# The memory's mean squares by one-column products on TensorE instead of token-major loads

## Chip, cores and metric

The kernel runs on one core of a Trainium2 chip. The metric is the device time of one execution in microseconds. A time quoted here is the median of several runs; the profile belongs to one further execution, with its own time.

## The reference

A two-layer encoder over 1024 tokens of width 1024, with 256 memory tokens of the same width. Both layers read the memory through an RMS norm with a gain and one projection for keys and values:

```
def rmsnorm(x, g):
    y = x * rsqrt(mean(x * x, axis=-1) + EPS)
    return y * g

memn = rmsnorm(mem, mem_norm_gain)
for l in range(DEPTH):
    h = rmsnorm(x, norm_gain[l])
    mk, mv = split(memn @ w_mem_kv[l])      # 4 heads of 128 each
    ...                                     # projections of h, attentions, gate, output projection
return rmsnorm(x, final_norm_gain)
```

The part that matters here is the mean of `mem * mem` over the 1024 features, one number for each of the 256 memory tokens.

## The kernel before

The kernel is written against a framework that allocates tiles from pools and orders each engine's queue ahead of time. A pool tag has a fixed number of buffers (`xt` has three, `x` six, `wraw`, `wh` and `wl` four, the PSUM bank `tr` three); a new tile of a tag waits until the oldest one has been read for the last time. Each engine works off its queue in order. Loads are issued by SP, one queue for all of them, which stops when its next load has to wait for a buffer.

All of the change lies in the preparation, `project_a`, the first 130 us or so. Matmuls work on operands that are split into a high part and a rest (`wh` and `wl`, `ah` and `al`, `H`), three products for one. What happens there, in the order of the program:

- `quarter(q, ...)` loads the input feature-major, 256 tokens at a time, in four loads of 128 x 512 (two blocks of 128 features), and splits each with its gain (ACT makes the high part, DVE the rest). Quarters 0 to 3 are the tokens of x, quarter 4 is the memory, from `mq`.
- `a_unit` (L864) multiplies a quarter by the first weights; four units, one for each quarter, with no norm applied yet.
- `mem_keys` (L568) multiplies the memory by the key weights of layer 0 in two PSUM banks, `pj` and then `tr`, each from four weight tiles. `wparts` loads such a tile into `wraw`; ACT makes `wh` from it and DVE `wl`.
- `mem_values` (L597) does the same for the values.
- `rstd(io["mt"], ...)` (L814, L815) computes the memory's norm: the memory is loaded a second time, token-major, in four tiles of 128 x 512 (`xt`), ACT squares each with a sum along the row, DVE adds the two halves, and `inv_sqrt` makes `rs_m`. The norm is applied after the products, when the banks of keys and values are read.
- `a_weights(1)` loads the next weights, the first two tiles of them into `x` buffers; `stats` does for x what `rstd` does for the memory, with eight tiles of `xt` for each half of x.

A loop of the same kind as the new one stands at L283 (`rstd_cols`), much later: the squares' sum over features is a product with the column `inv_d`, which holds 1/1024.

The queues around the place are not written by hand: the framework's scheduler sets them from its own estimates of time, so a change at one place moves rows at others.

Of the kernel before, what the change touches and what calls it, by code (L numbers as in the profile page):

```python
# [12 lines left out]
AF = mybir.ActivationFunctionType  # L13
OP = mybir.AluOpType
# [5 lines left out]
D = 1024  # L20
KT = 8
MEM = 256
EPS = 1e-6
# [41 lines left out]
class Trunk:  # L65
# [881 lines left out]
    def project_a(self, qa, ks, v, qd, mem_h, kvd):  # L947


        nc, tc, io = self.nc, self.tc, self.io  # L950

        def quarter(q, parts, kps=range(4)):
            for kp in kps:
                x = self.st("x", [128, 2, 256], pool=self.xp)
                src = io["xq"][q, kp] if q < 4 else io["mq"][kp]
                loaded = nc.sync.dma_start(x, src.rearrange("p (a n) -> p a n", a=2))
                for i in range(2):
                    kt = 2 * kp + i
                    self.with_gain(x[:, i, :], kt + (0 if q < 4 else 16), *parts(kt))
            return loaded  # L960

        def tokens(q):
            return lambda kt: tuple(t[kt][:, q * 256:(q + 1) * 256] for t in self.h)
        late = []

        def after(end):

            late.append(end)
            if len(late) > 1:
                flush()  # L970

        def flush():
            with tc.issue_after(self.last.ins):
                late.pop(0)()

        warm = self.st("rp", [128, 512], F32R)
        self.st("so", [128, 512])
        self.st("rt1", [128, 512])
        nc.gpsimd.memset(warm.bitcast(F32), 0.0)
        nc.scalar.activation(self.rs_m, warm.bitcast(F32)[:, :2], AF.Sqrt)  # L980
        p = [self.ps("pj") for _ in range(2)]
        for i in range(9):
            nc.tensor.matmul(p[i % 2], warm[:, :128], warm, start=True, stop=True)
        w0, w1m = io["w_mem0"], io["w_mem1"]
        mem_l = self.st("mem", [128, KT, MEM], F32R, pool=self.xp)
        mem = [[t[:, i, :] for t in mem_h for i in range(4)], [mem_l[:, i, :] for i in range(KT)]]
        ws = self.a_weights(0, lambda kp: quarter(0, tokens(0), [kp]))
        units = []
        for q in range(4):
            units.append(self.a_unit(ws, q))  # L990
            if q < 3:
                quarter(q + 1, tokens(q + 1))
        self.loaded = quarter(4, lambda kt: (mem[0][kt], mem[1][kt]))
        for q, a in enumerate(units):
            units[q] = self.st("x", [128, 2, 256], pool=self.xp)
            self.copy(units[q], a)
        self.wsplit = ("act", "dve")
        end = [self.mem_keys(w0, mem, kvd[0], ("pj", "tr"), "so", "rt1")]
        self.wsplit = ("act", "both")
        end.append(self.mem_values(w0, mem, kvd[0], "so"))  # L1000
        self.rope_tables()
        vm = self.st("xv", [128, 2])
        self.loaded = self.raws[6]
        self.rstd(io["mt"], [0, 1], vm, self.rs_m)
        self.wsplit = ("act", "dve")
        w1 = self.a_weights(1)
        self.stats(range(4))
        self.loaded = None
        self.along_columns(self.rows_m, self.rs_m)
        for e in end:  # L1010
            e()
        for q in range(2):
            after(self.k_unit(units[q], q, ks, v))
        self.mem_keys(w1m, mem, kvd[1], ("tr", "tr"), "so", "rt1")()
        self.stats(range(4, 8))
        for q in range(2, 4):
            after(self.k_unit(units[q], q, ks, v))
        for q in range(4):
            after(self.q_unit(self.a_unit(w1, q), q, 0, qa, qd))
        w2 = self.a_weights(2)  # L1020
        self.along_columns(self.rows, self.rs)
        for q in range(4):
            after(self.q_unit(self.a_unit(w2, q), q, 2, qa, qd))
            if q == 1:
                self.mem_values(w1m, mem, kvd[1], "so")()
        while late:
            flush()
        return self.mem_q(io["w_e"], E_QM)
# [1142 lines left out]
def _perm():  # L2171
    t = np.arange(T).reshape(16, 8, 8)
    return t.transpose(1, 0, 2).reshape(-1)


def _constants():
    c = {"c_ident": np.eye(128, dtype=np.float32)}

    t = _perm()
    freqs = np.power(np.float32(10000.0), -np.arange(16, dtype=np.float32) / np.float32(16)).astype(np.float32)  # L2180
    cos = np.zeros((T, 64), np.float32)
    sin = np.zeros((T, 64), np.float32)
    for a, pos in ((0, t // 64), (32, t % 64)):
        ang = (pos.astype(np.float32)[:, None] * freqs).astype(np.float64)
        cos[:, a:a + 16] = cos[:, a + 16:a + 32] = np.cos(ang)
        sin[:, a:a + 16] = -np.sin(ang)
        sin[:, a + 16:a + 32] = np.sin(ang)
    cos, sin = cos[:, _HALVES], sin[:, _HALVES]
    c["c_cos"] = cos.reshape(8, 128, 64).transpose(1, 0, 2).copy()
    c["c_sin"] = sin.reshape(8, 128, 64).transpose(1, 0, 2).copy()  # L2190
    return c
# [7 lines left out]
def layout(i):  # L2199
    a = {k: np.asarray(v) for k, v in i.items()}  # L2200
    perm = _perm()
    x = a["x"][0]
    d = _constants()
    d["xT"] = np.ascontiguousarray(x[perm].T).reshape(8, 128, T)
    d["xt"] = x[perm].reshape(8, 128, D)
    d["mt"] = a["mem"][0].reshape(2, 128, D)
    d["mq"] = a["mem"][0].T.reshape(4, 2, 128, MEM).transpose(0, 2, 1, 3).reshape(4, 128, 2 * MEM)
    g = np.concatenate([a["norm_gain"].reshape(16, 128), a["mem_norm_gain"].reshape(8, 128),
                        a["final_norm_gain"].reshape(8, 128)])
    d["gains"] = np.ascontiguousarray(g.T)  # L2210
    d["w_e"] = _tiles(a["w_in_even"][0])
    d["w_o"] = _tiles(a["w_in_odd"][0])
    rows = lambda w: w.reshape(12, 128, D)[list(ROWS)].reshape(-1, D)
    wv = a["w_in_odd"][0][:, 128 * O_V:128 * O_QM]
    d["w_v"] = wv.reshape(KT, 128, 2, 512).transpose(2, 0, 1, 3)
    d["w_oe"] = _tiles(rows(a["w_out_even"][0]))
    d["w_oo"] = _tiles(rows(a["w_out_odd"][0]))
    d["w_mem0"] = _tiles(a["w_mem_kv"][0])
    d["w_mem1"] = _tiles(a["w_mem_kv"][1])
    g = [a[nm][0] for nm in ("k_norm_a", "q_norm_a")]  # L2220
    d["g_kq"] = np.stack([v for u in g for v in (u, u.reshape(2, 2, 16)[:, ::-1].reshape(64))])[None][:, :, _HALVES]
    d["sink_b"] = a["sink_b"].reshape(1, 8)


    rel = np.arange(384)[None, :] - 128 - np.arange(128)[:, None]
    n = np.abs(rel)
    nf = np.maximum(n, 1).astype(np.float32)
    large = 8 + (np.log(nf / np.float32(8)) / np.float32(np.log(16.0)) * np.float32(8)).astype(np.int32)
    bucket = np.where(rel > 0, 16, 0) + np.where(n < 8, n, np.minimum(large, 15))
    padded = lambda t: np.concatenate([t, np.full((len(t), 1), NEG, np.float32)], 1)  # L2230
    d["band"] = padded(a["rel_bias"].T)[:, np.where(n <= 128, bucket, 32)]
    p = np.arange(128)
    r, cc = p // 8, p % 8
    start = np.clip(r - 4, 0, 8)
    row = (r[None, :] >= start[:, None]) & (r[None, :] < start[:, None] + 8)
    at = np.zeros((128, 5, 128), np.int64)
    for i, (b, k) in enumerate(((7, 6), (3, 2), (3, 3), (3, 4), (0, 1))):
        cq, ck = 8 * b + cc, 8 * k + cc
        start = np.clip(cq - 8, 0, 48)
        ok = row & (ck[None, :] >= start[:, None]) & (ck[None, :] < start[:, None] + 16)  # L2240
        at[:, i] = np.where(ok, (7 - r[:, None] + r[None, :]) * 31 + 15 - cq[:, None] + ck[None, :], 15 * 31)
    d["offsets"] = padded(a["rpb_c"][0].reshape(16, 15 * 31))[:, at]

    d["xq"] = d["xT"].reshape(4, 2, 128, 4, 256).transpose(3, 0, 2, 1, 4).reshape(4, 4, 128, 512)
    we = a["w_in_even"][0]
    halves = lambda w: w.reshape(D, -1, 64)[:, :, _HALVES].reshape(D, -1)
    wa = np.concatenate([halves(we[:, 128 * E_KA:128 * E_VA]), we[:, 128 * E_VA:128 * E_QB],
                         halves(we[:, :128 * E_KA])], 1)
    d["w_a"] = wa.reshape(4, 2, 128, 3, 256).transpose(3, 0, 2, 1, 4).reshape(3, 4, 128, 512)
    return {k: np.ascontiguousarray(v) for k, v in d.items()}  # L2250
# [17 lines left out]
```

## Time and profile before

| | |
|---|---|
| runs | 1478.82, 1481.55, 1482.13 us (median 1481.55) |
| profiled execution | 1482.22 us, span 1480.4 us, mean granted clock 0.998 |
| TensorE (PE) busy | 1461.3 us, 8049 matmuls |
| DVE, ACT, GpSimd (POOL) busy | 1038.8, 839.2, 647.0 us |
| moved by DMA | 271.87 MB, of which 174.28 MB read from HBM |

Times in the profile are microseconds from the start of the span, L12 is line 12 of the kernel. A row of a timeline has the start, the duration, engine, line, operation, the tile written and the tiles read, and in brackets how long the engine had been idle before it and what ended that. In the lists of waits the columns are the total, the number of waits and the longest. "PEld" is the loading of a matmul's stationary operand, which runs beside the matmuls.

### The profile page before, as it was taken

How to read it: one execution, taken by the hardware profiler on the slowest of the kernel's cores; microseconds unless marked ns; L12 is line 12 of the kernel's file. 1: busy time of each engine (PE TensorE's matmuls, PEld its weight loads, DVE VectorE, ACT ScalarE, POOL GpSimd, SP SyncE). 2: the span in 40 equal slices, each digit the busy share in tenths (PEclk: the TensorE clock that was granted, in tenths of full speed). 3: DMA queues.
4: the chain of work that ended last, by engine and by line, in shares of the span. 5: the costliest groups of instructions: out<-in, count | busy, mean ns of one | idle time of the engine just before them, and what ended most of it. 6: DMA issues, size and time to landing. Idle time of an engine off the chain costs nothing.

```text
span 1480.4 us, 24751 instructions
## 1 busy us (share of the span) xinstructions
PE 1461.3 (99%) x8049; PEld 1254.1 (85%) x8049; DVE 1038.8 (70%) x2125; ACT 839.2 (57%) x1877; POOL 647.0 (44%) x766
## 2 busy tenths in 40 slices
PE   9999999999999999999999999999999999999997
PEld 8898888888888888888888887888888888888776
DVE  6687777777776678776687866654457787778584
ACT  7743665556655466655454544444456777776454
POOL 1223658566775656553450000002425556665355
PEclk9999999999999999999999999999999999999999
DMA  8966335334342524378553343567675568778844
GB/s 282 314 161 184 117 114 168 122 122 132 117 144 79 199 75 139 110 263 313 182 180 135 136 136 139 156 171 256 225 257 169 187 198 270 246 250 313 306 132 150
DMA packets 171809, 271.87 MB, mean 184 GB/s; under 512 B 15648, under 2 KB 92704, under 8 KB 170656
## 3 DMA queue, kind: packets, MB, share of 16 engines
q1 hardware_dynamic: 171248, 270.20, 56.6%
q8 instruction: 64, 1.05, 0.3%
q14 instruction: 65, 0.53, 0.1%
q10 hardware_dynamic: 432, 0.09, 0.0%
HBM read 174.28 MB, written 83.89 MB: 174 GB/s over the span
## 4 chain that ended last, share of the span: by engine, by line
PE 87%; DMA 4%; DVE 4%; ACT 2%; issue 1%; SPq 1%; POOL 0%; DVEq 0%; ACTq 0%; POOLq 0%
PE pj L242 16%; PE pj L62 12%; PE x L1650 7%; PE tr L133 6%; PE pv L1080 4%; PE y L1650 4%; PE pv L62 3%; PE s L62 3%; PE sa L1348 3%; PE tr L62 3%; PE pj L1348 2%; PE pv L1650 2%; PE sa L1046 2%; PE sa L1047 2%; PE s L1348 2%; PE tr L1348 2%
## 5 line engine op out<-in xcount | busy, mean ns | idle before, releaser
L549 DVE TENSOR_TENSOR pl<-tr,ph 128x512 fp32r<-128x512 f32 (+2 forms) x352 | 204.3, 594 | 45.2 <-ACT ph L125 43.3
L242 PE MATMUL pj<-H,wh 128*128 128x512 f32 x704 | 233.4, 412 | 0.4 <-DVE vt L313 0.2
L125 ACT ACTIVATE ph<-tr 128x512 fp32r<-128x512 f32 (+2 forms) x352 | 176.8, 523 | 99.6 <-PE tr L133 77.8
L158 POOL TENSOR_SCALAR wh<-wraw 128x512 fp32r<-128x512 f32 x48 | 30.4, 636 | 268.0 <-PE x L1650 233.2
L125 ACT ACTIVATE wh<-wraw 128x384 fp32r<-128x384 f32 (+1 forms) x163 | 89.2, 554 | 98.5 <-PE pj L1348 11.8
L242 PE MATMUL pj<-H,wl 128*128 128x512 f32 x352 | 139.0, 395 | 0.0
L242 PEld LDWEIGHTS pj<-H,wh 128*128 128x128 f32 x704 | 120.2, 189 | 18.2 <-issue 0.6
L62 PE MATMUL pj<-H,wh 128*128 128x512 f32 x384 | 121.0, 396 | 0.0
L1133 POOL TENSOR_SCALAR pn<-pn,st 128x384 f32<-128x384 f32 (+1 forms) x128 | 72.9, 572 | 99.3 <-DVE st L1132 57.5
L133 PE MATMUL tr<-ident,P 128*128 128x128 f32 x752 | 115.3, 273 | 0.8 <-DVE pl L549 0.5
L1295 POOL TENSOR_TENSOR wl<-wraw,wh 128x384 fp32r<-128x384 f32 x56 | 63.5, 1135 | 89.7 <-ACT wh L125 78.7
L1131 ACT ACTIVATE pn<-pn,st 128x384 f32<-128x384 f32 (+1 forms) x128 | 75.1, 587 | 40.4 <-DVE st L1128 38.9
L133 PEld LDWEIGHTS tr<-ident,P 128*128 128x128 f32 x752 | 88.8, 140 | 9.5 <-DVE pl L549 1.8
L1052 ACT ACTIVATE P<-sa,st 128x1024 f32<-128x1024 f32 x64 | 71.5, 1117 | 34.4 <-DVE st L1051 16.9
L1054 POOL TENSOR_SCALAR P<-P,st 128x1024 f32<-128x1024 f32 x64 | 73.8, 1155 | 27.5 <-DVE st L1053 27.2
L1051 DVE TENSOR_REDUCE st<-sa 128x1 f32<-128x1024 f32 x64 | 77.5, 1218 | 8.0 <-PE sa L1047 7.4
L62 PE MATMUL s<-k,q 128*128 128x384 f32 (+1 forms) x352 | 81.4, 327 | 0.7 <-DMA k<-k 0.7
L242 PEld LDWEIGHTS pj<-H,wl 128*128 128x128 f32 x352 | 66.2, 188 | 15.2
L62 PE MATMUL pj<-H,wl 128*128 128x512 f32 x192 | 75.6, 394 | 0.0
L160 POOL TENSOR_TENSOR wl<-wraw,wh 128x512 fp32r<-128x512 f32 x52 | 71.3, 1373 | 9.6 <-ACT wh L125 7.2
L62 PEld LDWEIGHTS pj<-H,wh 128*128 128x128 f32 x384 | 66.6, 188 | 5.4
L864 PE MATMUL pj<-ah,H 128*128 128x256 f32 x384 | 70.7, 282 | 0.3 <-ACT ah L125 0.2
(574 smaller groups left out, 4170.0 us busy)
## 6 DMA issues: line engine op xcount, KB each, us to landing
y<-yb SPq DMA_DIRECT2D x24, 512.0 KB, 3.9
wraw<-s SPq DMA_DIRECT2D x64, 192.0 KB, 3.8
wraw<-w_e SPq DMA_DIRECT2D x44, 256.0 KB, 3.5
k<-k SPq DMA_DIRECT2D x42, 256.0 KB, 5.5
s<-bias SPq DMA_DIRECT2D x56, 192.0 KB, 2.0
wq<-w_o SPq DMA_DIRECT2D x40, 256.0 KB, 3.3
y<-sg SPq DMA_DIRECT2D x18, 512.0 KB, 3.5
wraw<-w_o SPq DMA_DIRECT2D x36, 256.0 KB, 4.3
```

The costliest lines, as they stand in the source:

```text
L62: return lambda *a, **k: self.tc.keep_in_program_order(getattr(self.engine, name)(*a, **k))
L125: return self.nc.scalar.activation(out, in_, AF.Copy, scale=scale)
L133: self.turned = self.fence = self.pe.transpose(o, i, self.ident)
L242: self.pe.matmul(a[:, :n], s[:, kt % UNIT, :], m, start=(kt == 0 and i == 0), stop=(kt == KT - 1 and i == 2))
L549: self.low = nc.vector.tensor_tensor(pl[:, :n], tr[:, :n], ph[:, :n], op=OP.subtract)
L1051: nc.vector.tensor_reduce(st[:, 0:1], s, axis=AX.X, op=OP.max, negate=True)
L1052: nc.scalar.activation(pt, s, AF.Exp, bias=st[:, 0:1], accum_out=st[:, 1:2])
L1054: self.normal = nc.gpsimd.tensor_scalar(pt, pt, st[:, 2:3], 0.5, op0=OP.mult, op1=OP.mult)
L1131: nc.scalar.activation(o, o, AF.Exp, bias=st[:, 0:1], scale=-1.0, accum_out=st[:, 2:3])
L1133: self.normal = normal = nc.gpsimd.tensor_scalar(o, o, st[:, 3:4], 0.5, op0=OP.mult, op1=OP.mult)
L1348: last = nc.tensor.matmul(bank, s[:, k, :], y[3 * u + k][m][:, cols], start=start and u + k + e == 0, stop=u == 1 and k + e == 4, skip_gro ...
L1650: self.last = nc.tensor.matmul(bank, ws[s][:, k, :], b[k][m], start=start and k + i == 0, stop=k == UNIT - 1 and i == 2, skip_group_check= ...
```

## The change

The squares are taken from the feature-major tiles of quarter 4: as each arrives, ACT squares it into an `xt` tile (no sum), and TensorE adds its two blocks into two columns of a `tr` bank by four products with `inv_d`, one for each block of 128 features and each 128 tokens. The sum over the four tiles is the mean. `rstd` on the memory is gone, with its four loads, four squares with sums, and two DVE operations; one DVE operation adds EPS from the bank. The token-major copy of the memory is no longer an input.

```diff
@@ project_a, quarter
                 loaded = nc.sync.dma_start(x, src.rearrange("p (a n) -> p a n", a=2))
+                if q == 4:
+                    sq = self.st("xt", [128, 512], pool=self.xp)
+                    nc.scalar.activation(sq, x.rearrange("p a n -> p (a n)"), AF.Square)
+                    for i in range(4):
+                        nc.tensor.matmul(mean[:, i % 2:i % 2 + 1], sq[:, i * 128:(i + 1) * 128], self.inv_d,
+                                         start=kp + i == 0, stop=kp == 3 and i > 1, skip_group_check=True)
                 for i in range(2):
@@ project_a
+        mean = self.ps("tr")
         self.loaded = quarter(4, lambda kt: (mem[0][kt], mem[1][kt]))
@@
         vm = self.st("xv", [128, 2])
         self.loaded = self.raws[6]
-        self.rstd(io["mt"], [0, 1], vm, self.rs_m)
+        nc.vector.tensor_scalar(vm, mean[:, :2], EPS, None, op0=OP.add)
+        self.inv_sqrt(vm, 2, self.rs_m)
@@ layout
-    d["mt"] = a["mem"][0].reshape(2, 128, D)
```

Lines behind the first piece stand 6 to 8 further down in the changed kernel; L959 is the new square, L961 the new product. The order of the queues differs throughout the preparation and is the same again from the first projections of layer 0 on. Three places matter.

SP's queue behind the cosine table of the rotary positions (`c_cos`; `c_sin` is the sine table). Before, with `mt` the token-major memory, `w_mem` the key and value weights, `xt` on the right the token-major x and `w_a` the next weights:

```order
L781 DMA rqn_778<-c_sin 128x512
L814 DMA xt_786<-mt 128x512
L814 DMA xt_789<-mt 128x512
L814 DMA xt_792<-mt 128x512
L138 DMA wraw_600<-w_mem 128x512
L138 DMA wraw_618<-w_mem 128x512
L138 DMA wraw_636<-w_mem 128x512
L814 DMA xt_795<-mt 128x512
L138 DMA wraw_654<-w_mem 128x512
L814 DMA xt_832<-xt 128x512
```

and now:

```order
L781 DMA rqn_803<-c_sin 128x512
L138 DMA wraw_625<-w_mem 128x512
L138 DMA wraw_643<-w_mem 128x512
L138 DMA wraw_661<-w_mem 128x512
L844 DMA x_817<-w_a 128x512
L138 DMA wraw_679<-w_mem 128x512
L844 DMA x_823<-w_a 128x512
L814 DMA xt_843<-xt 128x512
L814 DMA xt_846<-xt 128x512
L814 DMA xt_849<-xt 128x512
L814 DMA xt_852<-xt 128x512
L814 DMA xt_855<-xt 128x512
```

The four loads of the memory are gone, the weight tiles five to eight have moved up, and the tiles of w_a and the blocks of x follow at once.

ACT's queue from the square ahead of the fifth weight split (`wh` from `wraw`; before `wh_602`, now `wh_627`). Before:

```order
L815 ACTIVATE xt_792,xp_785<-xt_792 128x512
L125 ACTIVATE x_524<-pj_445 128x512
L125 ACTIVATE wh_602<-wraw_600 128x512
L815 ACTIVATE xt_795,xp_785<-xt_795 128x512
L125 ACTIVATE wh_620<-wraw_618 128x512
L792 ACTIVATE iq_t_800<-xv_784 128x2
L815 ACTIVATE xt_832,xp_831<-xt_832 128x512
L125 ACTIVATE wh_638<-wraw_636 128x512
```

and now:

```order
L959 ACTIVATE xt_533<-x_531 128x512
L125 ACTIVATE ah_819<-x_817 128x512
L125 ACTIVATE ah_825<-x_823 128x512
L815 ACTIVATE xt_843,xp_842<-xt_843 128x512
L792 ACTIVATE iq_t_811<-xv_809 128x2
L125 ACTIVATE wh_627<-wraw_625 128x512
L815 ACTIVATE xt_846,xp_842<-xt_846 128x512
L815 ACTIVATE xt_849,xp_842<-xt_849 128x512
L815 ACTIVATE xt_852,xp_842<-xt_852 128x512
L125 ACTIVATE wh_645<-wraw_643 128x512
L815 ACTIVATE xt_855,xp_842<-xt_855 128x512
L125 ACTIVATE wh_663<-wraw_661 128x512
```

Two splits of w_a and the square of a block of x now stand ahead of the fifth weight split, and three more squares ahead of the sixth. Further on, the squares of two more blocks (`xt_861`, `xt_864`) stand ahead of the first split for the values, `wh_701`.

TensorE's queue at the end of the last `a_unit` (`pj_445`) now has three of the four rows of products there, ahead of the first memory keys (`wh_554` is the first weight tile); the fourth row comes nine matmuls later:

```order
L864 MATMUL pj_445<-ah_222,H_133 128x256
L961 MATMUL tr_494<-inv_d_67,xt_497 128x1 x4
L961 MATMUL tr_494<-inv_d_67,xt_509 128x1 x4
L961 MATMUL tr_494<-inv_d_67,xt_521 128x1 x4
L568 MATMUL pj_551<-q_141,wh_554 128x256
```

Before, the first key matmul followed the last L864 directly.

## Prediction

> **What bounds the kernel now.** I read the page first, then the stretches of the preparation, then what TensorE (PE) waits for there, and last the chain of waits and the queues around the place of the change.
>
> ```profile
> PE 1461.3 (99%) x8049; PEld 1254.1 (85%) x8049; DVE 1038.8 (70%) x2125; ACT 839.2 (57%) x1877; POOL 647.0 (44%) x766
> PE 87%; DMA 4%; DVE 4%; ACT 2%; issue 1%; SPq 1%; POOL 0%; DVEq 0%; ACTq 0%; POOLq 0%
> ```
>
> TensorE is busy for 99% of the span and carries 87% of the chain that ended last. So work added to it costs its full length, unless it lands where TensorE would have waited; and what is taken from another engine counts only as far as it shortens a wait of TensorE. Where are those waits? Columns of the next rows: busy time and instructions of each engine, granted clock, share of the DMA engines, GB/s.
>
> ```profile
> 29.00:45.00 16.00, 13.58 (x102) 12.24 (x101) 5.58 (x13) 10.02 (x25) 6.38 (x5) 1.00 0.94 307
> 45.00:80.00 35.00, 34.64 (x244) 31.83 (x243) 24.40 (x70) 25.94 (x67) 8.21 (x7) 1.00 0.96 306
> 80.00:150.00 70.00, 68.94 (x462) 61.97 (x461) 55.65 (x131) 27.06 (x55) 23.92 (x21) 1.00 0.65 169
> ```
>
> From 29 to 45 us TensorE loses 2.4 us, in the 105 us after that 1.4. The clock is full. The DMA engines are 94 to 96% busy up to 80 us: here transfers, not arithmetic, decide when operands exist. What the waits between 29 and 150 us were for:
>
> ```profile
> PE tr L568 <- ACT wh L125: 1.7, 1, 1.7
> PE pj L597 <- DVE wl L160: 1.0, 3, 0.6
> PE tr L568 <- DVE wl L160: 0.4, 2, 0.2
> PE pj L597 <- ACT wh L125: 0.3, 1, 0.3
> PE pj L864 <- ACT ah L125: 0.2, 1, 0.2
> PE tr L133 <- POOL rp L898: 0.2, 1, 0.2
> ```
>
> The sum is 3.8 us: all that better feeding could give back here. The largest, 1.7 us, is the first matmul of the second bank of memory keys, which waits for ACT to split the fifth weight tile:
>
> ```profile
> 34.68 0.28 PE L568 MATMUL pj<-q,wl 128*128 128x256 f32 x1
> 36.66 0.39 PE L568 MATMUL tr<-q,wh 128*128 128x256 f32 x1 [1.71 <-ACT wh L125]
> 36.89 0.28 PE L568 MATMUL tr<-mem,wh 128*128 128x256 f32 x1
> 37.39 0.39 PE L568 MATMUL tr<-q,wl 128*128 128x256 f32 x1 [0.22 <-DVE wl L160]
> 37.61 0.28 PE L568 MATMUL tr<-q,wh 128*128 128x256 f32 x1
> 37.73 0.29 PE L568 MATMUL tr<-mem,wh 128*128 128x256 f32 x1
> ```
>
> (Matmuls of 256 columns start 0.12 us apart, as the last two rows show, so twelve of one weight tile take 1.4 us.) And why ACT is late there, in its own queue:
>
> ```profile
> 25.62 0.62 ACT L125 ACTIVATE wh<-wraw 128x512 fp32r<-128x512 f32 x1
> ...
> 31.89 0.63 ACT L815 ACTIVATE xt<-xt 128x512 f32<-128x512 f32 x1 [2.68 <-DMA xt<-mt]
> 32.58 0.63 ACT L815 ACTIVATE xt<-xt 128x512 f32<-128x512 f32 x1
> 34.89 0.63 ACT L815 ACTIVATE xt<-xt 128x512 f32<-128x512 f32 x1 [1.58 <-DMA xt<-mt]
> 35.99 0.62 ACT L125 ACTIVATE wh<-wraw 128x512 fp32r<-128x512 f32 x1
> 37.55 0.63 ACT L815 ACTIVATE xt<-xt 128x512 f32<-128x512 f32 x1 [0.94 <-DMA xt<-mt]
> 38.18 0.62 ACT L125 ACTIVATE wh<-wraw 128x512 fp32r<-128x512 f32 x1
> ```
>
> The fifth weight split (35.99) stands behind the squares of three token-major memory tiles, and these wait for their transfers. The chain of waits agrees:
>
> ```profile
> 24.43 7.44 DMA xt<-mt
> 31.89 0.73 ACT xt L815 x2
> 32.64 4.83 DMA xt<-mt
> ```
>
> So the loads that the change removes are just those that hold TensorE's largest wait. The question is what stands there in their place.
>
> **The change part by part.** One: the added products. Sixteen calls of one column, in the queue as four rows of x4. What one costs is seen at the other place that does this, L283, whose two calls of x4 the trace shows as x8:
>
> ```profile
> 742.74 0.95 PE L283 MATMUL pv<-inv_d,vt 128*128 128x1 f32 x8
> 743.55 1.03 PE L283 MATMUL pv<-inv_d,ph 128*128 128x1 f32 x8
> 744.44 0.71 PE L1348 MATMUL sa<-q,wh 128*128 128x512 f32 x2
> ```
>
> Eight records from 743.55 to 744.44 are 0.111 us each, two for a call; sixteen calls are 32 records, 3.6 us. Twelve of the calls stand directly ahead of the memory keys, where TensorE does not wait now (the keys follow the last L864 without a gap), four a little later. All 3.6 us therefore push the keys back: +3.6. It ends at 3.6 at most from these rows; at least 0 if TensorE would wait in any case, which is the next term. [...]
>
> Two: the squares move. Four squares leave ACT's queue at L815 and three of the new ones (L959, no accumulator) come in ahead of the first weight split, now at 25.62. A 128x512 operation on ACT lasts 0.62 us, so three push that split by 1.9 at most, to 27.5. TensorE, which comes to it after the twelve products, at 29.1 + 2.7 = 31.8, doesn't notice. Priced at nothing; were that cover gone, it would be 1.9. The first weight buffer comes free up to 1.9 us later, and so the fifth weight tile is issued by 29.5 instead of 27.6. That hides behind the DMA queue:
>
> ```profile
> 30.69 1.29 POOL L784 TENSOR_TENSOR c_cosk<-rt,so 128x512 f32<-128x512 f32 x1 [29.43 <-DMA rt<-c_cos]
> ```
>
> and in SP's queue:
>
> ```profile
> 23.25 0.44 SPq L781 DMA_DIRECT2D rt<-c_cos  x1
> 23.74 0.65 SPq L781 DMA_DIRECT2D rqn<-c_sin  x1
> 24.43 2.69 SPq L814 DMA_DIRECT2D xt<-mt  x3
> 27.62 2.60 SPq L138 DMA_DIRECT2D wraw<-w_mem  x3
> 32.64 0.33 SPq L814 DMA_DIRECT2D xt<-mt  x1
> ```
>
> The cosine table, issued at 23.25, is there only at 30.7, so what is issued up to 29.5 lands by its place in the queue.
>
> Three: the first wait. The four loads go, but ACT's queue now has the splits of two tiles of w_a and the square of the first block of x (xt_843) ahead of the fifth weight split. In SP's queue that block is the seventh transfer behind the sine table. The seventh before was the fourth memory tile, and its square began at 37.55. I take the same: square from 37.5, weight split from 38.2, done at 38.8. TensorE comes there at 34.8 + 3.6 = 38.4 and waits 0.4 instead of 1.7: -1.3. It ends at -1.7 (no wait) and at +0.6 (if that block, issued near 32, takes the 7.44 us of the first memory tile, it lands at 39.4, and TensorE starts at 40.7, 2.3 late).
>
> Four: the new wait. The sixth weight split now stands behind the squares of three more blocks of x, the last of which, xt_852, has to go into the buffer that xt_843 leaves, because xt has three. SP can't issue it before 38.2. How long it takes:
>
> ```profile
> DMA to landing us min/median/max: 3.8/4.8/8.1
> ```
>
> ```profile
> x<-P SPq DMA_DIRECT2D x12, 256.0 KB, 2.8
> ```
>
> The first row is of the xt tiles in the full queue of this stage, the second the same size in a quiet one. Here SP's queue is held behind xt_852, so the engines run dry and I take 2.8: landed at 41.0, square to 41.7, split to 42.3. TensorE is through the fifth tile at 38.8 + 1.4 + 0.5 (its usual pause for wl) = 40.7, so it waits 1.6. With 4.8 it would wait 3.6; nothing if ACT and transfers ran 1.6 earlier. The next two blocks have been issued meanwhile and follow closely: no wait. The seventh and eighth blocks again need buffers just freed, ahead of the first split for the memory values; by the same count ACT is done with that at 47.2, TensorE's keys at 47.0, and DVE's wl comes 0.7 after: +0.8 where now it is 0.3, so +0.5 (0 to +2.5). Together +2.1.
>
> Five: two small DVE operations fall away and one reads PSUM instead, off the path: 0, since rows_m is needed only after the keys. The three "tr" banks shift by one with the new bank in front, and that bank is read long before its turn comes again: 0. From layer 0 on, the order of all engines is as before. The waits between 45 and 150 us for wl, ah and rp stand in a changed order; all of them together are 1.4 us. I take 0, between -1.4 and +1.4.
>
> Sum: 3.6 - 1.3 + 2.1 = +4.4 us. The profiled execution took 1482.2, the median of the runs is 1481.55, 0.7 below, so the forecast from the median is 1481.55 + 4.4, rounded to **1486 us**.
>
> **The rivals.** *Better feeding hides the products (no change).* One MB less in a queue that is the limit; if the blocks of x follow each other without the pause that lies between the squares at 32.58 and 34.89, xt_843 is there at 36, the first wait goes altogether, and the buffer cycle ends before TensorE needs it: 3.6 - 1.7 - 0.4 = +1.5, 1483. For it speaks the DMA share; against it that ACT's queue asks for more bytes ahead of the same split than before.
>
> *The chain gets shorter (faster).* From 24.43 to 61 us the chain of waits runs through transfers and ACT, and TensorE joins it only then. One MB at 307 GB/s is 3.4 us; if TensorE at 61 us really hangs on that chain, everything behind moves forward by 3.4: 1478.1. It decides if the added 3.6 us fit into the waits ahead of 61 us. They are 2.4 us up to 45 and 0.4 up to 80, which is why I give it little.
>
> *The buffer cycle runs at the pace of the full queue (slower still).* With 4.8 us per turn, the wait of part four is 3.6 and the second one 2.5, after a first of 0.4: 3.6 - 1.3 + 3.6 + 2.2 = +8.1, 1489.7. For it speaks the median of 4.8; against, that SP stands still.
>
> [...]
>
> **How the numbers follow.** A measurement of this kernel can tell about 0.2%, 3.0 us, from no change, so "same" is 1478.6 to 1484.5. Chances: the forecast 0.48, the slower cycle 0.17, four passes 0.01, no change 0.27, the shorter chain 0.07. The forecast's own range is 1483.5 to 1489; 0.02 of its chance lies below 1484.5, and of the shorter chain 0.02 ends within 0.2%, so same has 0.27 + 0.02 + 0.02 = 0.31, slower 0.46 + 0.17 + 0.01 = 0.64 and faster 0.05. The range from 1481 to 1491 leaves out the shorter chain and the worst of the cycle, and adds the 1.4 us of part five on either side of the cases within it.
>
> **What would show it.** Right: 32 records of 128x1 near 29 us, 0.11 apart; ACT squares of x, not of the memory, just ahead of the fifth and sixth weight splits; TensorE's wait at the second bank of keys below 1 us and a new one of 1 to 3 us twelve matmuls later; from 150 us on the same spacing, only shifted. Wrong: if TensorE passes the keys and values without waits, so that the shift at 150 us is below 3 us; if the records are packed closer than 0.11; or if the shift at 150 us is not the difference of the spans.

## The result and the profile after

| | before | after |
|---|---|---|
| median | 1482.09 us (1478.82 to 1487.56, 7 runs) | 1491.42 us (1488.12 to 1495.78, 7 runs) |
| profiled execution, span | 1482.22, 1480.4 us | 1491.42, 1489.6 us |
| mean granted clock | 0.998 | 0.994 |

The ratio of the times is 1.0058, with a 95% interval of 1.0043 to 1.0073: slower, by 9.3 us, where +4.4 was forecast. The sign came out as said; about 5 us come from something that the sum did not have. The rows of the page that answer to those of before (instructions of each engine, shares of the chain of waits):

```profile
PE 1470.2 (99%) x8081; PEld 1264.6 (85%) x8081; DVE 1039.7 (70%) x2124; ACT 837.4 (56%) x1873; POOL 647.0 (43%) x766
PE 89%; DVE 4%; DMA 3%; ACT 1%; issue 1%; POOL 0%; SPq 0%; DVEq 0%; POOLq 0%; ACTq 0%
```

8081 matmuls are 32 more than before, as counted: two records for a call. TensorE's busy time has grown by 8.9 us, though, and not by 3.6. Where, is in the same stretches as before (busy time and instructions of PE, PEld, DVE, ACT and POOL, then granted clock, DMA share, GB/s):

```profile
29.00:45.00 16.00, 16.00 (x99) 16.00 (x99) 6.11 (x11) 7.86 (x20) 6.72 (x5) 0.68 0.68 230
45.00:80.00 35.00, 30.84 (x188) 26.63 (x188) 23.40 (x67) 24.41 (x61) 8.86 (x7) 0.95 0.86 264
```

The clock column had 1.00 in both before. Now it is 0.68 from 29 to 45 us, in a stretch in which TensorE is busy without a break (16.00 of 16.00) and yet executes 99 matmuls, not 102 and 32 on top. The DMA share fell from 0.94 to 0.68: the queue that was the limit now stands still more often, for buffers that come free later (the list of its waits follows below). TensorE's timeline in that stretch:

```profile
28.80 3.20 PE L961 MATMUL tr<-inv_d,xt 128*128 128x1 f32 x24
31.86 0.56 PE L568 MATMUL pj<-q,wh 128*128 128x256 f32 x1
32.22 0.41 PE L568 MATMUL pj<-mem,wh 128*128 128x256 f32 x1
32.44 0.41 PE L568 MATMUL pj<-q,wl 128*128 128x256 f32 x1
...
33.93 1.70 PE L961 MATMUL tr<-inv_d,xt 128*128 128x1 f32 x8
...
41.17 0.28 PE L568 MATMUL pj<-q,wl 128*128 128x256 f32 x1
41.29 0.28 PE L568 MATMUL pj<-q,wh 128*128 128x256 f32 x1
...
42.70 0.28 PE L568 MATMUL tr<-q,wh 128*128 128x256 f32 x1
```

The first row is the twelve calls ahead of the keys; within it the records start 0.111 us apart up to 31.0 us, and 0.214 apart from there on. The next eight need 1.6 us (33.93 to 35.49), and the key matmuls around them start 0.21 us apart (32.22, 32.44), not 0.12 as before. At 41.2 the spacing is 0.12 again. So TensorE ran at half speed from 31.0 to 41.2 us, 10.2 us long. From the first product to the second bank of keys (42.70, at `tr`) it took 13.9 us; at full speed 32 records of 0.111 and four weight tiles of 1.4 are 9.2. The clock cost 4.7 us here.

What TensorE still waited for between 29 and 150 us (another 0.2 us was for `wl`), and, from the list for SP's queue in the stretch from 28 to 45 us, the three waits that are longer than before (the first was 0.9 us, the others were not there):

```profile
PE tr L133 <- POOL rp L898: 2.3, 1, 2.3
PE pj L597 <- ACT wh L125: 1.9, 4, 1.3
```

```profile
SPq L138 <- DVE wl L160: 5.0, 4, 2.8
SPq L814 <- ACT iq_t L792: 2.4, 1, 2.4
SPq L814 <- PE tr L961: 1.7, 1, 1.7
```

The 1.7 us at the second bank of keys are gone, and so is any wait for the sixth weight split. New is the wait for the first rotated keys, `rp`. The chain of waits shows how it comes about, and TensorE's row behind it that the clock fell once more:

```profile
34.13 1.51 PE tr L961 x8
35.66 2.47 DMA xt<-xt
40.52 4.29 DMA xt<-xt
46.78 5.31 DMA xt<-xt
55.75 4.41 DMA xt<-xt
70.24 1.60 POOL rp L898
```

```profile
71.89 0.69 PE L133 MATMUL tr<-ident,rp 128*128 128x128 f32 x2 [2.31 <-POOL rp L898]
...
72.59 0.41 PE L568 MATMUL tr<-mem,wh 128*128 128x256 f32 x1
72.80 0.41 PE L568 MATMUL tr<-q,wl 128*128 128x256 f32 x1
```

A block of x is loaded only when TensorE has made the last products, because they are the last readers of the square in its `xt` buffer; SP's queue stands still for 1.7 us meanwhile. From there the chain goes through four turns of `xt` to the sum `rp`, which began at 59.53 us before, as the same view of POOL has it, and at 70.24 now:

```profile
59.53 0.97 POOL L898 TENSOR_TENSOR rp<-rt,rt 128x256 f32<-128x256 f32 x1 [3.31 <-DVE rt L895]
```

### The profile page after: what moved, and what is told of

Read it like the earlier page. It is cut to its first block, busy times and chain, and to the rows that moved or that the text cites. A ratio compares the mean times of both kernels' runs of the same rounds, so it can differ in the third digit from the quotient of the medians.

```text
span 1489.6 us, 24813 instructions
## 1 busy us (share of the span) xinstructions
PE 1470.2 (99%) x8081; PEld 1264.6 (85%) x8081; DVE 1039.7 (70%) x2124; ACT 837.4 (56%) x1873; POOL 647.0 (43%) x766
## 4 chain that ended last, share of the span: by engine, by line
PE 89%; DVE 4%; DMA 3%; ACT 1%; issue 1%; POOL 0%; SPq 0%; DVEq 0%; POOLq 0%; ACTq 0%
PE pj L242 15%; PE pj L62 12%; PE x L1658 7%; PE tr L133 6%; PE pv L1088 4%; PE y L1658 4%; PE pv L62 4%; PE s L62 3%; PE tr L62 3%; PE pj L1356 3%; PE sa L1356 3%; PE pj L864 2%; PE pv L1658 2%; PE s L1356 2%; PE sa L1054 2%; PE sa L1055 2%
## 5 line engine op out<-in xcount | busy, mean ns | idle before, releaser
L1139 ACT ACTIVATE pn<-pn,st 128x384 f32<-128x384 f32 (+1 forms) x128 | 75.1, 587 | 40.2 <-DVE st L1136 38.7
L864 PE MATMUL pj<-ah,H 128*128 128x256 f32 x384 | 71.3, 283 | 0.0
```

The lines of the kernel that those rows point to most:

```text
L864: self.last = nc.tensor.matmul(a[:, b * 256:(b + 1) * 256], x[kt][:, t], w, start=(kt + b + i == 0), stop=(kt == KT - 1 and i == 2), skip_ ...
L1139: nc.scalar.activation(o, o, AF.Exp, bias=st[:, 0:1], scale=-1.0, accum_out=st[:, 2:3])
```

## The experiments

Two theories stood against each other. T1, the clock: a run of some 3 us of one-column matmuls makes the granted clock fall, and it is the half speed behind them that costs. T2, the queues: whatever delays TensorE in the scheduler's estimate moves blocks of x ahead of weight splits, and the waits for buffers, transfers and ACT cost. A difference is that of the medians, run on the same chip as its kernel before.

| run | difference | ratio, 95% interval | clock in 29 to 45 us |
|---|---|---|---|
| k1_thin | +17.1 | 1.0126, 1.0110 to 1.0143 | 0.84 |
| k2_wide | +7.3 | 1.0052, 1.0040 to 1.0064 | 1.00 |
| k5_thin_late | +15.1 | 1.0111, 1.0090 to 1.0131 | 0.79 |
| k6_wide_late | +7.7 | 1.0058, 1.0040 to 1.0075 | 0.94 |
| k3_noprod | +2.3 | 1.0017, 1.0008 to 1.0026 | 1.00 |
| k4_spread | +6.7 | 1.0052, 1.0039 to 1.0065 | 1.00 |
| k11_wide_double | +4.2 | 1.0031, 1.0020 to 1.0043 | 1.00 |
| k12_wide_once | +1.8 | 1.0016, 1.0007 to 1.0024 | 1.00 |
| k7_after_xlate | +5.3 | 1.0041, 1.0026 to 1.0057 | 0.89 |
| k8_pool_xlate | +2.3 | 1.0015, 1.0004 to 1.0026 | 0.79 |
| k9_pool_behind | +6.6 | 1.0043, 1.0027 to 1.0058 | 1.00 |
| k10_before_xlate | +6.3 | 1.0039, 1.0026 to 1.0052 | 1.00 |

### Thin and wide matmuls in the kernel before

k1_thin, ahead of the memory keys:

```diff
+        junk = self.ps("tr")
+        for i in range(16):
+            nc.tensor.matmul(junk[:, i % 2:i % 2 + 1], self.ident, self.inv_d, start=i == 0, stop=i > 13, skip_group_check=True)
```

> The kernel before (token-major loads and all) with sixteen one-column products of two constants, 32 records, into an unused bank, directly ahead of the memory keys. T1 (the clock): a stretch of one-column matmuls counts as little activity, and the granted clock falls behind them, as in the changed kernel, where 29 to 45 us had 0.68 and the key matmuls stood 0.213 us apart for some 10 us. Then here too: granted clock 0.65 to 0.8 in 29 to 45 us, key matmuls 0.21 apart for 7 to 10 us, and +4 to +8 us against the kernel before, with none of the changed kernel's loads. T2 (the queues of ACT and SP and the three xt buffers): the loads are those of before, so the clock stays at 1.00, the 3.6 us of products are partly taken up by the 1.7 us wait, and the time is +1.5 to +3.6. T3 (the products' own length alone): +3.6, clock 1.00.

+17.1 us, and by another way than either theory had. Half of the records, whose operands are constants, went ahead to 5 us. Here are the rest and what came behind, on TensorE:

```profile
29.86 1.84 PE L996 MATMUL tr<-inv_d,ident 128*128 128x1 f32 x16
...
31.76 0.28 PE L568 MATMUL pj<-mem,wh 128*128 128x256 f32 x1
31.88 0.28 PE L568 MATMUL pj<-q,wl 128*128 128x256 f32 x1
...
45.30 0.58 PE L568 MATMUL tr<-q,wh 128*128 128x256 f32 x1 [7.84 <-ACT wh L125]
...
46.48 0.41 PE L568 MATMUL tr<-q,wh 128*128 128x256 f32 x1
46.70 0.41 PE L568 MATMUL tr<-mem,wh 128*128 128x256 f32 x1
```

A run of 16 records, 1.7 us, left the clock as it was (keys 0.12 apart behind it). But ACT's fifth weight split was put behind five squares of x, TensorE waited 7.8 us for it, and behind this wait the keys stand 0.21 apart: half speed came behind a wait, too. The run tells nothing of a long thin run.

k2_wide, the same with matmuls of 256 columns:

```diff
+        for i in range(31):
+            nc.tensor.matmul(junk[:, :256], self.h[0][0][:, :128], self.h[0][0][:, :256], start=i == 0, stop=i == 30)
```

> The kernel before with 31 matmuls of 256 columns at the same place as in the run with thin products: by 0.117 us each, 3.6 us of TensorE time, at full activity. T1: the clock stays at 1.00, key matmuls 0.117 apart, and the time is +1.5 to +3.6, at least 3 us below the run with thin products. T2 and T3: the same time as the run with thin products, within 1.5 us.

+7.3 us, twice the upper end of T1's figure, with the clock at 1.00 and only 16 of the 31 left at the place. T2 is not empty: 1.9 us more on TensorE were enough to reorder loads and squares, and the waits between 29 and 150 us grew from 3.8 to 6.7 us.

k5_thin_late and k6_wide_late repeat the pair with an operand that arrives late, so that nothing goes ahead (the loop also stands a few lines further down, directly before `mem_keys`):

```diff
-            nc.tensor.matmul(junk[:, i % 2:i % 2 + 1], self.ident, self.inv_d,
+            nc.tensor.matmul(junk[:, i % 2:i % 2 + 1], mem[0][5][:, i % 2 * 128:i % 2 * 128 + 128].bitcast(F32), self.inv_d,
...
-            nc.tensor.matmul(junk[:, :256], self.h[0][0][:, :128], self.h[0][0][:, :256],
+            nc.tensor.matmul(junk[:, :256], mem[0][5][:, i % 2 * 128:i % 2 * 128 + 128], mem[0][5],
```

> The kernel before with sixteen one-column products of a memory tile that arrives late, so that all 32 records stand in one run directly ahead of the memory keys (in the earlier thin run half of them had gone ahead to 5 us, and 1.7 us were left there). T1 (the clock falls behind a run of about 3 us of one-column matmuls): granted clock 0.65 to 0.85 in 29 to 45 us, key matmuls about 0.21 us apart for 5 to 10 us, and at least 3 us slower than the run with as many wide ones, in all +9 to +14 against the kernel before. T2 (the queues: whatever delays TensorE in the scheduler's estimate draws blocks of x ahead of weight splits in ACT's queue, which then costs waits): clock 1.00, the time of the wide run within 1.5 us, +6 to +9.

> The kernel before with 31 matmuls of 256 columns of the same late memory tile at the same place, 3.6 us at full activity. Both theories: clock 1.00, key matmuls 0.117 apart. T1: at least 3 us below the thin run. T2: the thin run's time within 1.5 us; and 4 us or more over the kernel before although there are only 3.6 us of matmuls, since the blocks of x stand ahead of the weight splits as in the first wide run, with waits of 5 us or more for ACT's and DVE's splits between 29 and 150 us.

TensorE with the thin run, and then with the wide one (the first view begins at 28.9 us, behind the first of the 32 records):

```profile
28.74 4.36 PE L999 MATMUL tr<-inv_d,q 128*128 128x1 f32 x31
...
33.33 0.41 PE L568 MATMUL pj<-mem,wh 128*128 128x256 f32 x1
...
38.22 0.28 PE L568 MATMUL pj<-q,wh 128*128 128x256 f32 x1
38.34 0.28 PE L568 MATMUL pj<-mem,wh 128*128 128x256 f32 x1
```

```profile
30.25 3.87 PE L999 MATMUL tr<-q 128*128 128x256 f32 x31
...
41.69 0.39 PE L568 MATMUL tr<-q,wh 128*128 128x256 f32 x1 [1.92 <-ACT wh L125]
...
43.18 0.41 PE L568 MATMUL tr<-mem,wh 128*128 128x256 f32 x1
43.39 0.41 PE L568 MATMUL tr<-q,wl 128*128 128x256 f32 x1
...
46.53 0.28 PE L568 MATMUL tr<-mem,wh 128*128 128x256 f32 x1
```

As T1 says: half speed from 31.4 to 38.2 us with the thin run, none behind the wide one, and 7.5 us between the two medians, where T2 allowed 1.5. But +15.1 is above T1's range too, and the 6.8 us at half speed cost only about 3.4 of it; what makes up the rest of the 7.5 us was not shown. The wide run itself shows the loss that T2 named, +7.7 us for 3.6 us of matmuls, and one thing that neither expected: 1.9 us of waiting, up to 41.69, and behind it 3.4 us at half speed (43.0 to 46.4).

### The changed kernel without the thin run

k3_noprod keeps two products of sixteen, and so leaves out most of the mean:

```diff
-                    for i in range(4):
-                        nc.tensor.matmul(mean[:, i % 2:i % 2 + 1], ...)
+                    if kp == 3:
+                        for i in range(2):
+                            nc.tensor.matmul(mean[:, i:i + 1], ...)
```

> The changed kernel with two of the sixteen products (only the first of each pair of the last tile; it leaves out most of the mean). The squares, the missing token-major loads and the order of the blocks of x stay about as in the changed kernel. T1: clock 1.00 in 29 to 45 us, 6 to 9 us less than the changed kernel, so -1.5 to +3 against the kernel before; the waits for ACT's fifth and sixth weight split show up again at TensorE, 1 to 4 us together, now that it comes there early. T2: the loss is in the queues, so the time stays within 4 us of the changed kernel, +5 or more against the kernel before. T3: 3.2 us below the changed kernel, +6 against the kernel before.

+2.3 us at clock 1.00, as T1 said and against T2: 7 us of the 9.3 go with the products. The scheduler loaded two blocks of x earlier here, so it is not the products alone that differ, and the waits for the fifth and sixth weight split that were expected at TensorE did not come. k4_spread makes one call behind each third key matmul:

```diff
+                        if between:
+                            kp, j, sq, product = between.pop(0)
+                            product(kp, j, sq)
```

> The changed kernel with the same sixteen products, but one call (two records) after every third key matmul in the first bank of keys, instead of rows of eight records on end. T1: no stretch of one-column work is long any more; the granted clock is 0.95 or more in 29 to 45 us and the time 3 to 6 us below the changed kernel, +2 to +6 against the kernel before. T2 and T3: as many products at the same place, so the changed kernel's time within 1.5 us, +7 to +10 against the kernel before.

+6.7 us, between the two forecasts. The clock stays at 1.00, as T1 has it, but TensorE's waits in the stretch are 7.7 us, of which 2.5 for weight splits of the values and 2.4 for `rp`; the queues had changed too. Undecided.

k11_wide_double was made to change nothing but the width of the products: the same number of records at the same two places, 256 columns wide. ACT writes the squares as fp32r.

```diff
-                    for i in range(4):
-                        nc.tensor.matmul(mean[:, i % 2:i % 2 + 1], sq[:, i * 128:(i + 1) * 128], self.inv_d, ...)
+                    for i in range(8):
+                        nc.tensor.matmul(mean[:, i % 2 * 256:i % 2 * 256 + 256], sq[:, i % 4 * 128:i % 4 * 128 + 128], inv[:, :256], ...)
...
+        inv = self.st("invw", [128, 256], F32R, pool=self.xp)
+        nc.gpsimd.memset(inv.bitcast(F32), 0.5 / D)
```

> The changed kernel with products of the same count of records, the same length and at the same places, but with 256 columns each: ACT writes the squares as fp32r, the column is widened to 256 equal columns of 1/2048, and each of the sixteen products is made twice, so that 24 records stand ahead of the keys and 8 nine matmuls later, each 0.117 us. The orders of SP and ACT up to the sixth weight split are nearly those of the changed kernel. T1 (the clock): 1.00 in 29 to 45 us, key matmuls 0.117 apart, 3 to 6 us less than the changed kernel, so +3 to +6 against the kernel before. T2 (queues and buffers alone): the changed kernel's time within 1.5 us, +8 to +11.

+4.2 us, 5.1 below the changed kernel, as T1 said. The stretch, and TensorE's timeline in it:

```profile
29.00:45.00 16.00, 15.22 (x120) 14.24 (x120) 5.57 (x11) 8.92 (x23) 6.61 (x5) 1.00 0.77 247
```

```profile
28.69 3.03 PE L961 MATMUL tr<-invw,xt 128*128 128x256 f32 x24
31.56 0.28 PE L568 MATMUL pj<-q,wh 128*128 128x256 f32 x1
31.67 0.28 PE L568 MATMUL pj<-mem,wh 128*128 128x256 f32 x1
...
38.54 0.39 PE L568 MATMUL tr<-q,wh 128*128 128x256 f32 x1 [0.21 <-ACT wh L125]
```

The wide records take about as long as the thin ones were forecast to (24 in 2.9 us), the keys stand 0.12 us apart, and the second bank starts at 38.54 with a wait of 0.2; the changed kernel was there at 42.70. One difference is left: the sixth weight split stands behind one square of x here, not three. TensorE did not wait for that split in the changed kernel, so the 4.7 us counted there from the spacing don't hang on it. The 5.1 us between the runs can: behind three squares the split would have ended at about 41.9 us here, the time of the third square's end (41.2) and 0.6, and TensorE wants it at about 40.2, so an estimated 1.7 us of the 5.1 may be that difference.

k12_wide_once makes each wide product once, with 1/1024 in the columns (`range(4)`, `1.0 / D`).

> As the run with doubled wide products, but each product once (16 records, 1.9 us, 1/1024). The scheduler now lets blocks of x and weight splits alternate. T1 and T2 together: clock 1.00, 1.9 us of products, waits of TensorE between 29 and 150 us of 2 to 5 us, so -1 to +4 against the kernel before, and at least 1.5 us below the doubled one. If the place in the queue decides and not the length: the same as the doubled one.

+1.8 us, 2.4 below the doubled one for 1.9 us less of matmuls: what lies ahead of the keys costs about its full length, as far as a pair can tell in which the queues differ too. This is the best form of the change that was found, and it is still not faster than the kernel before.

### Holding back the blocks of x

k7_after_xlate is one line of the changed kernel:

```diff
-        self.loaded = self.raws[6]
+        self.loaded = self.raws[13]
```

> The changed kernel with one edit: the blocks of x are held back until the second weight tile of the values has been issued, so that the weight splits stand ahead of their squares in ACT's queue. The products stand as in the changed kernel, 24 records and then 8. T1: the clock is below 0.8 in 29 to 45 us, key matmuls 0.21 apart for about 10 us, and the time at least +6 against the kernel before, less than 3 us below the changed kernel. T2: the loss was in the queues, so it goes back to +3.6 or less, with waits of TensorE below 3 us in all between 29 and 150 us. If both act: 0.68 in the clock and +4 to +7.

+5.3 us, within the range named for both acting, above T2's bound and below T1's; the clock of 0.89 fits none of them. It fell behind the same 24 + 8 records, but for 3.4 us only (33.8 to 37.2), so the same run of products does not always cost the same. In this profile TensorE is an estimated 3.8 us late at 150 us (1024 matmuls done, 32 of them new, for the 1008 of before; 16 at some 0.235 us). The mean clock of the whole execution is 0.995, and the 3.4 us here with the some 4.5 us at half clock at the end, as in the kernel before, would leave an estimated 0.997: half speed came again later, so the +5.3 is not the price of the preparation alone. k8_pool_xlate has the same hold and adds up the squares on POOL first:

```diff
+                    if kp:
+                        nc.gpsimd.tensor_tensor(total[0], total[0], sq, op=OP.add)
+                    else:
+                        total.append(sq)
+                    for i in range(4 if kp == 3 else 0):
```

> The changed kernel with the same hold on the blocks of x, and with the four squares added up on POOL first, so that four products (8 records, 0.9 us) are left of sixteen. T1: too short a run for the clock, so 1.00 in 29 to 45 us. Both theories: 0.9 us of products, waits of TensorE between 29 and 150 us below 3 us, so -2 to +2 against the kernel before. If the queues don't matter (T1 alone): the waits of the changed kernel stay, +3 or more.

+2.3 us, just above the forecast, and not for the reason given: the products stood amid the keys and waited for POOL, whose last addition stood behind the rotary tables.

```profile
37.77 1.87 PE L965 MATMUL tr<-inv_d,xt 128*128 128x1 f32 x8 [3.70 <-POOL xt L961]
39.50 0.56 PE L568 MATMUL pj<-q,wl 128*128 128x256 f32 x1
```

Eight records need 1.73 us behind that wait, 0.22 each: half speed, behind a wait of 3.7 us. k9_pool_behind takes the wait away by moving the products behind the last key:

```diff
+        mean = self.ps("tr")
+        for i in range(4):
+            nc.tensor.matmul(mean[:, i % 2:i % 2 + 1], total[0][:, i * 128:(i + 1) * 128], self.inv_d, ...)
```

> As the run with the squares added up on POOL and the blocks of x held back, but the four products stand behind the last memory key, so that no key waits for POOL's sum (3.7 us at 33.8 there, behind which the clock was halved), and the sum stands in an rt1 buffer. T1 and T2 together: 8 records behind the keys and no wait before them, clock 1.00 from 29 to 45 us, waits of TensorE of 1 to 4 us between 29 and 150 us, so 2 to 5 us below that run, -4 to +1 against the kernel before: what is left of the gain from 1 MB less to load. If the wait for POOL had only taken the place of others (the transfers decide): the same as that run, +1 to +4.

A miss: the clock is at 1.00 in 29 to 45 us, but the time is +6.6 us, higher than with the wait. k10_before_xlate, the hold alone in the kernel before, shows the same:

> The kernel before with the hold alone: its token-major memory tiles and the blocks of x stand behind the second weight tile of the values. No products. T2: the 1.7 us wait at the second bank of keys goes, the waits of TensorE between 29 and 150 us fall from 3.8 us to 1 to 3, clock 1.00, -3 to 0 against the kernel before. If the order of these loads doesn't matter, or if the norm of the memory now comes too late for the keys' banks: 0 to +4.

+6.3 us, a miss as well. In both runs the loss is at the end of the preparation, first k9_pool_behind, then k10_before_xlate:

```profile
132.19 0.66 PE L133 MATMUL tr<-ident,rp 128*128 128x128 f32 x4 [2.94 <-POOL rp L898]
134.21 2.07 PE L242 MATMUL pj<-H,wh 128*128 128x512 f32 x4 [1.37 <-ACT wh L125]
```

```profile
130.17 0.66 PE L133 MATMUL tr<-ident,rp 128*128 128x128 f32 x4 [0.89 <-POOL rp L898]
135.05 2.07 PE L242 MATMUL pj<-H,wh 128*128 128x512 f32 x4 [4.22 <-ACT wh L125]
```

Waits of 4.3 and 5.1 us that the kernel before doesn't have, and behind them matmuls of 512 columns 0.43 us apart instead of 0.23: half speed again. In these two runs, holding the blocks of x back only moves the loss. Why the first weight split of layer 0's projections comes so late there was not followed up.

## Why the prediction was right and wrong

*The forecast.* Slower, by 4.4 us; measured +9.3. The likeliest case had the right sign, and the median lies 5.4 us above its figure, 0.4 above the upper end of the range; the kernel before had itself moved from 1481.55 to 1482.09 us. With the clock left alone (k11_wide_double) the number comes out, +4.2, but in part by luck: the wait of 1.6 us for the sixth split is in the sum and not in that run. The mean granted clock of the seven runs was 0.994 to 0.997, and 0.998 before; the missing share times the span gives an estimate of 1.5 to 6 us that half speed cost beyond its cost before, 4 on average. So the profiled run, with 6, is one that lost much to the clock, and about 5 us of the 9.3 are left for the sum.

*Part one, the products: the step that failed.* Number and spacing were right: 32 records, two for a call, 0.111 us apart up to 31.0 us. Wrong was to price the products by their own length alone. "The clock is full" was read from the stretches before and carried over to a stretch that the change itself fills with other work. The rows of L283 that gave the price show 16 records on end (1.7 us) with the clock at 1.00; nothing of before shows 24 on end. The term was 3.6 and should have been 3.6 + 4.7. The slow stretches lasted 10.2 us (changed kernel), 6.8 (k5_thin_late) and 3.4 (k7_after_xlate, k6_wide_late), so the price was not the same from run to run; what sets the length was not shown. In the changed kernel no gap at all went before the first fall, in k6_wide_late one of 1.9 us.

*Where the clock changed.* In the trace of the changed kernel the granted clock changes at 30.89, 41.13, 71.86 and 75.27 us: half for 10.24 us, full for 30.73, half for 3.41, which are some 3, 9 and 1 times the last. The first fall came 2.1 us behind the start of the one-column records (28.80). In k7_after_xlate the same run starts at 28.81; the spacing is still 0.12 us at 33.56, behind all 32 records, and 0.21 from 33.99 on. Why the clock fell later there was not shown. In k11_wide_double the wide records start at 28.69 us, 0.1 us from where the thin ones do, so the time at which the run starts is no rival for the difference of these two.

*Part two, the squares.* Priced at nothing; TensorE has no wait for the first splits. Right.

*Parts three and four, ACT's queue.* ACT kept the times of the forecast within 0.4 us:

```profile
37.64 0.63 ACT L815 ACTIVATE xt<-xt 128x512 f32<-128x512 f32 x1
...
38.37 0.61 ACT L125 ACTIVATE wh<-wraw 128x512 fp32r<-128x512 f32 x1
...
41.37 0.63 ACT L815 ACTIVATE xt<-xt 128x512 f32<-128x512 f32 x1 [1.16 <-DMA xt<-xt]
42.00 0.62 ACT L125 ACTIVATE wh<-wraw 128x512 fp32r<-128x512 f32 x1
```

The square of xt_843 was put at 37.5, the fifth split at 38.2, the square of xt_852 at 41.0, the sixth split done at 42.3. But TensorE, at half speed, came to the second bank at 42.70 and waited for neither: the terms +0.4 and +1.6 lie inside the slow stretch, so the wait of 1 to 3 us that was named as a sign of being right did not come. At the values it waits 1.9 us for ACT's splits where it had 0.3, +1.6 for the +0.5 of the sum, within its bounds of 0 to 2.5. Overlooked was that the products, too, hold `xt` buffers: SP's queue waits 1.7 us for the last of them.

*Part five, the rest.* Taken as 0, within 1.4 either way. The `rp` wait alone went from 0.2 to 2.3 us; with the waits for `wl` and `ah` the rest grew by 0.7, from 1.8 to 2.5, which the bounds allow. Half speed behind the `rp` wait (0.95 over 35 us, so about 1.7) is outside them. The measured terms together, 3.6 + 4.7 for the products, -1.7 for the first wait, +1.6 at the values, +0.7 and +1.7 here, are 10.6 us, and at 150 us the same matmul stands 10.6 us later than before.

*The rivals.* The slower buffer cycle (1489.7) is nearest by its number, and not the mechanism: no wait at the sixth split. Better feeding shows as the wait that went, but did not hide anything. No run shows the four passes that have 0.01 in the chances: sixteen calls made 32 records, two each.

*Same spacing later.* Not quite, by the prediction's own sign. At L283 the shift is 10.5 us (742.74 and 753.23), at the end of the span 9.2. Where the 1.3 us went was not looked into.

```profile
753.23 0.95 PE L283 MATMUL pv<-inv_d,vt 128*128 128x1 f32 x8
```

*How long a run, how long a wait.* Behind 16 one-column records on end, 1.7 us, the clock stayed full (L283, k1_thin); with 24 in 3.1 us it fell (changed kernel). It stayed full behind waits of 1.71 us (the kernel before) and 1.8 (k5_thin_late, for `rp`), and half speed followed on waits of 1.9 (k6_wide_late) and 2.3 (changed kernel). These are single cases; where the limit lies, and that there is one, was not shown.

*What stays open.* What makes the changed kernel spread over 7.7 us was not shown; the kernel before spreads over 8.7 in its own seven runs. How wide a matmul has to be for the clock to stay full was not tried between 1 and 256 columns.

## What to carry to other kernels

When a change puts narrow matmuls in a row on a busy TensorE, price what they do to the clock behind them, not only their own length: here 4.7 us on top of 3.6. A wait can have the same second price: in k6_wide_late 3.4 us at half speed followed on one of 1.9 us. A one-column f32 product here took two records of 0.111 us, a 256-column fp32r one a single record of 0.12 (24 in 2.9 us, k11_wide_double), and the wide form left the clock at 1.00 there, 5.1 us below the changed kernel, so try a wider moving operand. And where a scheduler sets the queues, an experiment that adds time at one place moves the rest: compare pairs that add the same time.

## What the runs showed of the hardware

- Busy is not full speed: with TensorE at 16.00 of 16.00 us (29 to 45 us, changed kernel) the granted clock was 0.68, with 24 one-column records in 3.1 us at the start.
- In the changed kernel a one-column f32 record took 0.111 us at full and 0.213 at half clock; a 256-column matmul of the keys 0.117 and 0.213.
- Half speed followed on waits of 1.9 us (k6_wide_late), 2.3 (changed kernel, 71.89), 3.7 (k8_pool_xlate), 4.2 (k10_before_xlate) and 7.8 (k1_thin), the first two for 3.4 us.
- Half speed lasted 10.24 and 3.41 us in the changed kernel, and about 6.8 us in k5_thin_late and 3.4 in k7_after_xlate by the spacing of the matmuls.
